# Hybrid mixer and mixture of experts on one core: six gates in other places, another order in routing, an extra slot of 64 places

## The chip, the cores and the metric

One core of a Trainium2 chip runs the whole program. The metric is the device time of one execution in microseconds (us); lower is better. The engines are named as in the profile: PE is TensorE (PEld its weight loads), DVE is VectorE, ACT is ScalarE, POOL is GpSimd, and SP issues most of the DMAs.

## The reference, cut to what matters

512 tokens of 1024 values go through a first block (which the change leaves alone) and a second one. The second has a mixer with three branches, each under a gate, and 16 experts of which each token uses two.

```python
def second_block(...):
    h = rms_norm(x, g_norm1) * (1 + sc1) + sh1
    x = x + gt1 * hybrid_mixer(h, ...)
    h2 = rms_norm(x, g_norm2) * (1 + sc2) + sh2
    return x + gt2 * hier_moe(h2, ...)

def hybrid_mixer(h, ...):                      # proj = h @ w_in, split into the parts below
    y_a = gmlp_branch(gelu(a_u), gelu(a_v), ...)  # u * (w_s @ layer_norm(v) + b_s), chunks of 128
    o_b = gla_scan(g_q, g_k, g_v, log_alpha)      # gated linear attention
    y_b = rms_norm(o_b, gla_norm_g) * silu(g_r)
    y_c = dsa_attention(q, k, d_v, d_iq, d_ik, d_iw, rel_bias)   # top 128 keys by an indexer
    up = einsum('nbse,ned->bsnd', [y_a, y_b, y_c], w_branch)
    gate = sigmoid(gates + b_branch_gate)         # 3 gates of 1024 columns, from h alone
    return sum(gate * up) @ w_out

def hier_moe(hf, ...):       # 4 groups of 4 experts: the best group, in it the best two experts
    for each expert:         # gate and up: 1024 -> 256 each, down: 256 -> 1024
        y += (silu(hf @ wg) * (hf @ wu) * weight) @ wd
```

## The kernel before, in words

**Products.** All large products are made in split precision: an fp32 operand is cut into a high half (a copy on ScalarE, L155 for weights) and a low half (a subtraction on VectorE, L156), and three matmuls add up hi*hi, lo*hi and hi*lo (L170 to L172). A product of 1024 rows and 128 columns for all 512 tokens, `gemm`, is 24 matmuls of 512 columns. `gemmA` (L971) is the same for 512 columns at once, with four PSUM tiles, one for each 128 tokens. A few small products are made in fp32, unsplit.

**Order.** Up to L1310 the order of the instructions on each engine is written by a planner when the program is built, from costs of its own and from the order in the program. From L1310 to the end of the experts the order on TensorE, VectorE and ScalarE is the program's own (`manual_schedule`); a call there that makes a weight's halves or a transpose's copy stands where it is written.

**Mixer.** The stretch runs from about 735 us to 1280 us of the span: the indexer and its top keys, the products for u, q and k, the product for v (`gemmA(A['wA'][0],ev_v)`, L1075), where `ev_v` normalises each block's rows (`gv`, L1074), and gMLP's mixing right behind it (`PE m L1078`). The attention follows (L1081 to L1105), a chain of small steps with little for TensorE. Then `merge(0)` adds gMLP's branch: for each of 8 column blocks d one gate (`gemm` of 24 matmuls, and a Tanh into the tile `th`, of which there are two) and one branch product of 12 matmuls, added into `merged[d]`. The gates need h alone, so the planner uses them, and with gMLP's branch products, as work for TensorE while the attention's chain runs. GLA comes next: its products, then seven levels of small matmuls (`gla_level`, L1140 to L1168), each behind a chain over VectorE (`kp`, `qp`) and ScalarE. `merge(2)` (the attention's branch) and `merge(1)` (GLA's) end the mixer, and the product with w_out's first half follows.

**Routing.** The second half of w_out goes by blocks of 128 tokens in the loop of L1345. Each block has four `product` calls of 6 matmuls; `x2half` adds them to x and sums the squares, `inverse` makes the inverse root, `turned`, `logits` and `added` bring the half's router logits of the block before, each over TensorE and another engine. `rows_out` writes a block's normalised rows, scaled by a2 (1 + sc2 times the weight), to `d_h2` in DRAM. For blocks 0 and 1, d_h2 has been filled with the shift sh2 long before (L1038), and POOL adds the rows by an accumulating DMA; for blocks 2 and 3, VectorE adds the shift row `sh2r` itself and SP writes them. After the loop the last block's three steps and its `rows_out` come, then the top-two choice, the ranks (`rps`), the one-hot tiles `Ak` and the token lists `idx`, all on VectorE with few matmuls. The gather (L1467) then fetches the first expert's rows from d_h2.

**Experts.** Each of 17 slots has 128 places: slots 0 to 15 are the experts' own, slot 16 is the extra one, for the expert with more than 128 tokens, if any. A slot transposes its gathered rows (L1473), splits them, makes the up products (`up_piece`, 4 pieces, 24 matmuls, 512 columns: 256 of the gate and 256 of up), Silu (L1488) times up, a transpose and the down products (`down`: 6 split matmuls and 2 fp32 ones), and adds its rows to the output by an indirect DMA of POOL's. Each expert's weights are 6 pieces of 512 KB, fetched by SP in the order of `todo` into 26 buffers (`slots`) as these come free, and split in the order of `pieces`, three pieces ahead of their use. What goes into the extra slot is found by `further` (slots 3 to 7) and `extra(0)` (slot 11). The last slots run in the order 15, 16, the end of slot 15 within slot 16's products. At the end a register `nx` decides whether a tail with six more slots runs (L1565), which is when more than one extra slot is needed.

## Time and profile before

| what | value |
|---|---|
| median of 3 runs | 1489.78 us (1485.41 to 1494.95) |
| profiled execution, its own time | 1490.69 us |
| its span in the trace | 1488.9 us |
| mean granted TensorE clock | 0.979 |
| TensorE (PE) busy | 1423.3 us, 96% |
| VectorE (DVE) busy | 1028.4 us, 69% |
| ScalarE (ACT) busy | 642.4 us, 43% |
| GpSimd (POOL) busy | 94.9 us, 6% |
| DMA | 226.16 MB, mean 152 GB/s |

The span runs from the first to the last instruction that the trace shows; the execution's own time is 1.8 us longer. Busy shares are means over the whole span. The granted clock is the share of TensorE's full clock that the chip let it run at. A line of the view of busy time by stretch has the stretch (start and end in us), its length, the busy us and the instructions of PE, PEld, DVE, ACT and POOL, then the granted clock, the DMA engines' busy share and their GB/s.

### The profile page before, as it was taken

The page shows a single profiled execution, that of the slowest core. Times are in us where ns is not written, and L with a number is a line of the kernel's source. Part 1 is how long each engine was busy: PE and PEld are TensorE (multiplying, and loading weights), DVE is VectorE, ACT ScalarE, POOL GpSimd, SP SyncE. Part 2 cuts the span into 40 slices and gives each one's busy share as a digit, 9 for nine tenths or more (in the row PEclk, how much of TensorE's full clock was granted, in tenths as well). Part 3 has the DMA queues.
Part 4 walks back from the last instruction along what each step waited for, and adds up shares of the span by engine and source line. Part 5 has one row for each costly group of instructions (what it writes and reads, how often), then busy time and mean ns, then how long its engine had stood idle before and what let it go on. Part 6 is the DMA issues. An engine that isn't in the chain of part 4 may idle for free. (4 is left out here: it accounts for less than half of the span.)

```text
span 1488.9 us, 22888 instructions
## 1 busy us (share of the span) xinstructions
PE 1423.3 (96%) x8863; PEld 1107.0 (74%) x8863; DVE 1028.4 (69%) x1948; ACT 642.4 (43%) x1045; POOL 94.9 (6%) x114
## 2 busy tenths in 40 slices
PE   9999998999999999999999989999899999599996
PEld 5777877677777787778777777777678887377774
DVE  6788977578777767544749867654544344789995
ACT  6554374234443443223443324463622333266663
POOL 0121000000000000000001000000000000123321
PEclk9999998999999999999999999999999999799999
DMA  5347234143556535553424211222044234499992
GB/s 215 134 154 251 85 112 133 66 142 124 167 177 212 183 115 188 172 170 114 146 99 140 92 57 50 64 95 80 23 167 138 92 127 165 142 391 362 331 342 58
DMA packets 78885, 226.16 MB, mean 152 GB/s; under 512 B 19571, under 2 KB 20211, under 8 KB 78771
## 3 DMA queue, kind: packets, MB, share of 16 engines
q1 hardware_dynamic: 68626, 201.79, 39.0%
q0 software_dynamic: 8992, 19.71, 4.8%
q10 hardware_dynamic: 1152, 3.15, 0.5%
q8 instruction: 71, 1.16, 0.3%
q14 instruction: 44, 0.35, 0.1%
HBM read 208.06 MB, written 27.03 MB: 158 GB/s over the span
## 5 line engine op out<-in xcount | busy, mean ns | idle before, releaser
L155 ACT ACTIVATE hi<-raw 128x1024 fp32r<-128x1024 f32 (+1 forms) x181 | 181.1, 1001 | 395.6 <-PE g L171 255.2
L156 DVE TENSOR_TENSOR lo<-raw,hi 128x1024 fp32r<-128x1024 f32 (+1 forms) x181 | 208.1, 1150 | 203.5 <-ACT hi L155 202.9
L172 PE MATMUL g<-bh,lo 128*128 128x512 f32 x376 | 152.4, 405 | 2.6 <-DVE lo L156 2.4
L170 PE MATMUL g<-bh,hi 128*128 128x512 f32 x376 | 152.1, 405 | 0.0
L171 PE MATMUL g<-bl,hi 128*128 128x512 f32 x376 | 150.3, 400 | 0.0
L170 PE MATMUL g<-hh,hi 128*128 128x512 f32 x336 | 133.1, 396 | 0.0
L172 PE MATMUL g<-hh,lo 128*128 128x512 f32 x336 | 132.7, 395 | 0.2 <-DVE lo L156 0.2
L171 PE MATMUL g<-hl,hi 128*128 128x512 f32 x336 | 132.6, 395 | 0.0
L172 PEld LDWEIGHTS g<-bh,lo 128*128 128x128 f32 x376 | 71.5, 190 | 22.6 <-DVE lo L156 4.1
L170 PEld LDWEIGHTS g<-bh,hi 128*128 128x128 f32 x376 | 71.7, 191 | 19.3 <-issue 2.4
L171 PEld LDWEIGHTS g<-bl,hi 128*128 128x128 f32 x376 | 71.4, 190 | 16.2 <-issue 0.2
L170 PE MATMUL g<-xh,hi 128*128 128x512 f32 x192 | 76.8, 400 | 0.0
L170 PEld LDWEIGHTS g<-hh,hi 128*128 128x128 f32 x336 | 63.3, 188 | 17.7 <-ACT hi L155 2.5
L172 PE MATMUL g<-xh,lo 128*128 128x512 f32 x192 | 76.4, 398 | 0.0
L171 PE MATMUL g<-xl,hi 128*128 128x512 f32 x192 | 76.2, 397 | 0.0
L172 PEld LDWEIGHTS g<-hh,lo 128*128 128x128 f32 x336 | 63.3, 188 | 15.5 <-DVE lo L156 0.6
L171 PEld LDWEIGHTS g<-hl,hi 128*128 128x128 f32 x336 | 63.3, 189 | 14.6
L885 DVE SCALAR_TENSOR_TENSOR acc<-raw,ca,acc 128x1024 f32<-128x1024 f32 x42 | 53.8, 1282 | 28.7 <-DMA raw<-in_wmod 28.4
L914 DVE SCALAR_TENSOR_TENSOR c<-g,vec,c 128x511 f32<-128x511 f32 x88 | 65.6, 745 | 1.1
L777 PE MATMUL g<-hi,fh 128*128 128x512 f32 x136 | 53.9, 396 | 0.0
L779 PE MATMUL g<-lo,fh 128*128 128x512 f32 x136 | 53.7, 395 | 0.0
L778 PE MATMUL g<-hi,fl 128*128 128x512 f32 x136 | 53.7, 395 | 0.0
(705 smaller groups left out, 3200.7 us busy)
## 6 DMA issues: line engine op xcount, KB each, us to landing
raw<-in_wexp SPq DMA_DIRECT2D x89, 512.0 KB, 13.2
raw<-in_win SPq DMA_DIRECT2D x72, 512.0 KB, 3.5
raw<-in_wmod SPq DMA_DIRECT2D x48, 512.0 KB, 4.1
raw<-in_wup SPq DMA_DIRECT2D x44, 512.0 KB, 4.3
raw<-in_wdn SPq DMA_DIRECT2D x22, 512.0 KB, 3.9
raw<-in_wout SPq DMA_DIRECT2D x16, 512.0 KB, 4.8
ws<-in_wexp SPq DMA_DIRECT2D x13, 512.0 KB, 14.3
raw<-in_wA SPq DMA_DIRECT2D x12, 512.0 KB, 3.9
```

The source lines that it names most:

```text
L155: S.activation(hi[:,:f],raw[:,:f],AF.Copy)
L156: V.tensor_tensor(lo[:,:f],raw[:,:f],hi.bitcast(F32)[:,:f],op=OP.subtract)
L170: PE.matmul(ps,hi[:,sl],xh[k],start=(k==0),stop=False)
L171: PE.matmul(ps,hi[:,sl],xl[k],start=False,stop=False)
L172: PE.matmul(ps,lo[:,sl],xh[k],start=False,stop=(k==n-1))
L777: PE.matmul(ps,xh[k][:,sl],w[kk][0],start=(k==0),stop=False)
L778: PE.matmul(ps,xl[k][:,sl],w[kk][0],start=False,stop=False)
L779: PE.matmul(ps,xh[k][:,sl],w[kk][1],start=False,stop=(k==2*n-1))
L885: else: V.scalar_tensor_tensor(acc,raw,ca[:,k:k+1],acc,op0=OP.mult,op1=OP.add)
L914: for k in (1,2): V.scalar_tensor_tensor(c[:,k:],ps[:,:512-k],Vc(f'fw{2-k}',i),c[:,k:],op0=OP.mult,op1=OP.add)
```

## The change

**Gates.** The Tanh tiles number four in place of two (GA+1), and each gate is a function of its own, `gate(n,d)`. `merge` makes the gates up to three blocks ahead of the branch product that uses them. Gates 0 to 2 of gMLP's branch are written between the product for v and gMLP's mixing; gates 0 to 2 of the attention's branch are written within GLA's levels, ahead of levels 0, 2 and 4.

**Routing.** `d_h2` is filled with the shift for all four blocks, and all four are then added by POOL's accumulating DMA; the row sh2r is not loaded. `rows_out` of the block before and `added` stand between the two halves of the last `product` call; the last block's `rows_out` is a scaling on ScalarE and stands ahead of its `added`; only block 3 is scaled by a2 ahead (`scaled`). 13 matmuls of 512 columns whose result nobody reads, `keep_going(13)`, stand behind the product that makes the token lists.

**The extra slot** has 64 places and is computed in fp32, with two halves of its columns in two column groups of TensorE's array (`rows64`, `up64`, `end64`, `act64`, `down64`), its weights unsplit. It stands between slots 14 and 15. Finding its expert begins a slot earlier (`further` in slots 2 to 6), and `extra(0)` is in slot 9. `keep_going(5)` stands ahead of the last slot's transposes. The tail runs when more than one extra slot is needed or an expert has more than 192 tokens, and then has seven slots, the first for the places behind the 64 of the extra slot.

```diff
-    mpool=pool('mp',bufs=2,stack=ph2)
+    GA=3
+    mpool=pool('mp',bufs=GA+1,stack=ph2)
...
+    gates={}
+    def gate(n,d):
+        ps=gemm(w2b(23+8*n+d),hh,hl)
+        gates[n,d]=th=mpool.tile([128,512],F32,name='th',tag='th'); S.activation(th,ps,AF.Tanh,bias=bgh[:,8*n+d:8*n+d+1],scale=0.5)
...
-            ps=gemm(w2b(23+8*n+d),hh,hl)
-            th=mpool.tile([128,512],F32,name='th',tag='th'); S.activation(th,ps,AF.Tanh,bias=bgh[:,8*n+d:8*n+d+1],scale=0.5)
+            for d2 in range(d,min(8,d+GA)):
+                if (n,d2) not in gates: gate(n,d2)
+            th=gates[n,d]
...
-    with tc.issue_after(oh_.ins): nc.sync.dma_start(d_h2[0:256,:],bass.AP(tensor=d_mod.tensor,offset=d_mod.offset+3072,ap=[[0,256],[1,1024]]))
+    with tc.issue_after(oh_.ins): nc.sync.dma_start(d_h2,bass.AP(tensor=d_mod.tensor,offset=d_mod.offset+3072,ap=[[0,512],[1,1024]]))
...
     gemmA(A['wA'][0],ev_v); next(kn_)
+    for d in range(GA): gate(0,d)
     for g in range(4):
...
     for li,n in enumerate((1,2,4,8,16,32,64)):
+        if li<2*GA and li%2==0: gate(2,li//2)
         for j in range(2): gla_level(li,n,j)
...
-    for i in range(4):
+    for i in (0,2,3):
         m=pe_.tile([128,1024],F32,name='modr',tag=f'modr{i}'); modr.append(m)
         nc.sync.dma_start(m,bass.AP(tensor=d_mod.tensor,offset=d_mod.offset+2048+1024*i,ap=[[0,128],[1,1024]]))
-    gt1r,sh2r,a2r,gt2r=modr
+    gt1r,a2r,gt2r=modr
...
+    def product(tb,ps,p,kks=(0,1)):
         sl=slice(tb*128,tb*128+128); hi,lo=wl1[p]
-        for kk in range(2):
+        for kk in kks:
...
-        if tb<2:
+        if tb<3:
             h=pw.tile([128,1024],F32,name='h2',tag='h2'); V.scalar_tensor_tensor(h,x1t[tb],v,a2r,op0=OP.mult,op1=OP.mult)
-            G.dma_start(d_h2[tb*128:tb*128+128,:],h,accum_op=OP.add)
         else:
-            h=blk[tb]['h']; V.scalar_tensor_tensor(h,h,v,sh2r,op0=OP.mult,op1=OP.add)
-            nc.sync.dma_start(d_h2[tb*128:tb*128+128,:],h)
+            h=blk[tb]['h']; S.activation(h,h,AF.Copy,scale=v)
+        G.dma_start(d_h2[tb*128:tb*128+128,:],h,accum_op=OP.add)
     for tb in range(4):
         ps=pg.tile([128,512],F32,name='g',tag='g')
         product(tb,ps,0); product(tb,ps,1)
         if tb: turned(tb-1)
         product(tb,ps,2)
         if tb: logits(tb-1)
-        product(tb,ps,3)
-        if tb: added(tb-1)
+        product(tb,ps,3,(0,))
+        if tb: rows_out(tb-1); added(tb-1)
+        product(tb,ps,3,(1,))
         x2half(tb,1,ps)
         nc.scalar.dma_start(out[tb*128:tb*128+128,:],x1t[tb])
-        if tb: rows_out(tb-1)
+        if tb==3: scaled(tb)
         inverse(tb)
-        if tb>=2: scaled(tb)
-    turned(3); logits(3); added(3); rows_out(3)
+    turned(3); logits(3); rows_out(3); added(3)
...
+    def keep_going(n):
+        w=pt()
+        for _ in range(n): PE.matmul(w,trib[:,:128],Ak[:,0:4,:].rearrange('p i s -> p (i s)'),start=True,stop=True)
+    keep_going(13)
...
+        mc=pe_.tile([128,1],F32,name='mc'); V.tensor_reduce(mc,cnt,axis=AX,op=OP.max)
+        V.scalar_tensor_tensor(mc,mc,192.5,pos[:,47:48],op0=OP.is_gt,op1=OP.add)
+        V.tensor_copy(ei[:,0:7],EQ[:,0,0:7]); V.tensor_copy(ei[:,7:8],mc)
...
-    for s_ in range(1,17): pieces+=[(s_,p) for p in range(4)]+[(s_-1,4),(s_-1,5)]
-    pieces[-6:]=[(16,0),(16,1),(15,4),(15,5),(16,2),(16,3),(16,4),(16,5)]
+    for s_ in range(1,15): pieces+=[(s_,p) for p in range(4)]+[(s_-1,4),(s_-1,5)]
+    pieces+=[(16,p) for p in range(4)]+[(14,4),(14,5),(15,0),(15,1),(16,4),(16,5)]+[(15,p) for p in range(2,6)]
...
+    def rows64(xg):
+        xf=pe2.tile([128,8,64],F32,name='xf',tag='xgl',bufs=1)
+        for hf in range(2):
+            ps=pt((128,4,64))
+            for kk in range(4): PE.transpose(ps[:,kk,:],xg[:64,(4*hf+kk)*128:(4*hf+kk)*128+128],ident[:64,:64])
+            S.activation(xf[:,4*hf:4*hf+4,:],ps,AF.Copy)
+        return xf
+    h64=lambda e: slice(64*e,64*e+64)
+    def up64(ps,xf,p,raw):
+        for kk in range(2):
+            k=2*p+kk
+            for e in range(2): PE.matmul(ps[h64(e),:256],xf[:,k],raw[:,kk*512+256*e:kk*512+256*e+256],start=(k==0),stop=(k==7))
+    def end64(ps,wcol):
+        u=sq_pool.tile([64,256],F32,name='u64',tag='sq',bufs=3); V.tensor_scalar(u,ps[64:,:256],wcol[:64],None,op0=OP.mult)
+        a=sq_pool.tile([64,256],F32,name='a64',tag='sq',bufs=3); S.activation(a,ps[:64,:256],AF.Silu)
+        V.tensor_tensor(a,a,u,op=OP.mult); return a
+    def act64(a):
+        pT=pt((128,2,64))
+        for f in range(2): PE.transpose(pT[:,f,:],a[:,f*128:f*128+128],ident[:64,:64])
+        af=pe2.tile([128,2,64],F32,name='af64',tag='afx',bufs=1); S.activation(af,pT,AF.Copy)
+        return af
+    def down64(af,raws,ix):
+        y=pe2.tile([128,1024],F32,name='ye',tag='ye',bufs=3); ps=psum()
+        for f in range(2):
+            for e in range(2): PE.matmul(ps[h64(e)],af[:,f],raws[f][:,512*e:512*e+512],start=(f==0),stop=(f==1))
+        for e in range(2): V.tensor_tensor(y[:64,512*e:512*e+512],ps[h64(e)],gt2r[h64(e),512*e:512*e+512],op=OP.mult)
+        G.indirect_dma_start(out=out,out_offset=bass.IndirectOffsetOnAxis(ap=ix,axis=0),in_=y[:64],in_offset=None,
+                             bounds_check=511,oob_is_err=False,compute_op=OP.add)
...
+    for e in range(14):
         O=None
-        if e<13: xgs.append(gather(idx[:,e+4:e+5]))
-        if e==3: fur=further()
-        if 3<=e<8: next(fur,None)
-        if e==11: xps=pm.tile([128,17,8],F32,name='m',tag='m'); O=extra(0,xps,16)
-        if e==8:
+        if e<11: xgs.append(gather(idx[:,e+4:e+5]))
+        else: xgs.append([lambda:gather(idx[:64,16:17],64),lambda:gather(idx[:,15:16]),lambda:None][e-11]())
+        if e==2: fur=further()
+        if 2<=e<7: next(fur,None)
+        if e==9: xps=pm.tile([128,17,8],F32,name='m',tag='m'); O=extra(0,xps,16)
+        if e==7:
             e0=nc.values_load(ei[0:1,0:1],min_val=0,max_val=15,engines=[ET.SP])
-            w0=[(A['wexp'][bass.ds(e0,1),p].rearrange('o p f -> (o p) f'),p==5) for p in range(6)]
-            todo+=w0[:2]+wx(15,(4,5))+w0[2:]
-        if e<16: ps=psum(); up_piece(ps,xin,0,piece(e+1,0))
+            w0=[(A['wexp'][bass.ds(e0,1),p].rearrange('o p f -> (o p) f'),True) for p in range(6)]
+            todo+=w0[:4]+wx(14,(4,5))+wx(15,(0,1))+w0[4:]+wx(15,range(2,6))
+        ps=psum(); up_piece(ps,xin,0,piece(e+1,0))
         aa=act_in(a)
-        if e<16:
-            for p in range(1,4):
-                if e==15 and p==2: down(aa,piece(e,4),piece(e,5),idx[:,e:e+1])
-                up_piece(ps,xin,p,piece(e+1,p))
-            a=up_end(ps,wcl[:,e+1:e+2])
+        for p in range(1,4): up_piece(ps,xin,p,piece(e+1,p))
+        a=up_end(ps,wcl[:,e+1:e+2])
         if O: placed(*O)
-        if e<15: xin=rows_in(xgs[e+2],e+2)
-        if e!=15: down(aa,piece(e,4),piece(e,5),idx[:,e:e+1])
+        xin=rows_in(xgs[e+2],e+2) if e<13 else rows64(xgs[15])
+        down(aa,piece(e,4),piece(e,5),idx[:,e:e+1])
         if O: infos(xps,16,17,wcl,idx)
+    ps=psum()
+    for p in range(2): up64(ps,xin,p,piece(16,p))
+    aa=act_in(a)
+    for p in range(2,4): up64(ps,xin,p,piece(16,p))
+    a=end64(ps,wcl[:,16:17])
+    xin=rows_in(xgs[16],15)
+    down(aa,piece(14,4),piece(14,5),idx[:,14:15])
+    ps=psum(); up_piece(ps,xin,0,piece(15,0)); af=act64(a)
+    up_piece(ps,xin,1,piece(15,1))
+    down64(af,(piece(16,4),piece(16,5)),idx[:64,16:17])
+    for p in range(2,4): up_piece(ps,xin,p,piece(15,p))
+    a=up_end(ps,wcl[:,15:16]); keep_going(5)
+    down(act_in(a),piece(15,4),piece(15,5),idx[:,15:16])
...
-    nx=nc.values_load(ei[0:1,7:8],min_val=0,max_val=7)
+    nx=nc.values_load(ei[0:1,7:8],min_val=0,max_val=8)
     with tc.If(nx>1):
         xps=pm.tile([128,17,8],F32,name='m',tag='m')
         wc2=pe_.tile([128,17],F32,name='wc2'); ix2=pe_.tile([128,17],U32,name='ix2')
-        for j in range(1,7): placed(*extra(j,xps,j))
```

## Rows read from the trace of the kernel before

**Rows 1.** The page, part 1: busy us of each engine, share of the span, instructions.
```profile
PE 1423.3 (96%) x8863; PEld 1107.0 (74%) x8863; DVE 1028.4 (69%) x1948; ACT 642.4 (43%) x1045; POOL 94.9 (6%) x114
```

**Rows 2.** Busy time by stretch, three of 50 us.
```profile
500.00:550.00 50.00, 50.00 (x217) 40.56 (x216) 35.92 (x42) 20.48 (x28) 0.00 (x0) 1.00 0.49 159
850.00:900.00 50.00, 45.48 (x217) 35.65 (x216) 34.63 (x97) 13.91 (x20) 0.00 (x0) 0.93 0.18 58
1350.00:1400.00 50.00, 50.00 (x224) 37.46 (x224) 48.20 (x67) 34.19 (x52) 17.76 (x10) 1.00 0.99 349
```

**Rows 3.** Waits of TensorE, 870 to 900 us: us in total, times, longest.
```profile
PE m L1078 <- DVE gv L1074: 3.9, 2, 2.8
PE g L170 <- ACT yh L186: 0.5, 1, 0.5
```

**Rows 4.** Busy time by stretch, cut at waits and clock steps.
```profile
891.60:898.40 6.80, 5.20 (x17) 4.36 (x17) 5.56 (x12) 2.93 (x5) 0.00 (x0) 0.50 0.12 48
1031.90:1064.40 32.50, 26.62 (x902) 19.48 (x902) 26.49 (x69) 19.10 (x55) 0.00 (x0) 0.95 0.04 12
1065.70:1069.10 3.40, 3.40 (x15) 2.46 (x16) 2.32 (x3) 1.94 (x5) 0.00 (x0) 0.50 0.32 107
1299.40:1304.60 5.20, 5.17 (x15) 4.00 (x16) 3.13 (x14) 2.64 (x4) 0.99 (x1) 0.50 0.89 289
1304.60:1309.00 4.40, 4.40 (x27) 3.35 (x26) 4.06 (x6) 3.12 (x4) 0.00 (x0) 1.00 1.01 397
```

**Rows 5.** Timeline of VectorE (start us, us, what), within 1049 to 1068 us.
```profile
1062.38 1.22 DVE L156 TENSOR_TENSOR lo<-raw,hi 128x1024 fp32r<-128x1024 f32 x1
```

**Rows 6.** Waits of TensorE, 1030 to 1066 us.
```profile
PE m L1138 <- issue: 2.3, 2, 2.0
...
PE g L172 <- DVE lo L156: 1.8, 1, 1.8
```

**Rows 7.** Timeline of all engines in routing; brackets: idle before, and its releaser.
```profile
1279.77 0.24 DVE L1329 TENSOR_REDUCE l<-m 128x20 f32<-128x80 f32 x1 [0.88 <-PE m L1328]
...
1280.41 0.69 DVE L1279 TENSOR_TENSOR g<-g,modr 128x512 f32<-128x512 f32 x1
...
1286.12 1.28 DVE L1343 SCALAR_TENSOR_TENSOR h<-h,nv,modr 128x1024 f32<-128x1024 f32 x1
...
1287.32 0.23 DVE L1365 TENSOR_REDUCE mx<-lg 128x20 f32<-128x80 f32 x1
...
1294.96 1.19 POOL L1467 DMA_INDIRECT xg<-d_h,idx  x1 [17.45 <-DVE idx L1408]
...
1299.43 1.94 PE L1473 MATMUL m<-cst,xg 128*128 128x128 f32 x8 [5.84 <-DMA xg<-d_h,idx]
```

**Rows 8.** Answer on the tile d_h, 1269 to 1278 us.
```profile
L1341 POOL DMA_DIRECT2D d_h<-h x2: 864/890/916, 1270.0 to 1276.6; - x2
...
DMA to landing us min/median/max: 5.0/5.1/5.2
```

**Rows 9.** Timeline of TensorE, 0 to 8 us.
```profile
1.20 5.28 PE L278 MATMUL m<-zb 128*128 128x512 bf16 x17 [1.20 <-DVE o L276]
```

**Rows 10.** Timeline of ScalarE, 1317 to 1329 us.
```profile
1317.48 0.38 ACT L1488 ACTIVATE a<-g 128x256 f32<-128x256 f32 x1 [1.87 <-PE g L1486]
...
1327.29 0.38 ACT L1488 ACTIVATE a<-g 128x256 f32<-128x256 f32 x1 [1.88 <-PE g L1486]
```

**Rows 11.** Timeline of TensorE, 825.7 to 827.2 us.
```profile
825.76 0.40 PE L172 MATMUL g<-bh,lo 128*128 128x512 f32 x1
826.08 1.06 PE L200 MATMUL m<-sq,cst 128*32 128x512 f32 x6
827.07 0.51 PE L170 MATMUL g<-bh,hi 128*128 128x512 f32 x1
```

**Rows 12.** Timeline of TensorE, 1471.5 to 1479 us.
```profile
1472.55 0.44 PE L1493 MATMUL m<-cst,a 128*128 128x128 f32 x2 [0.99 <-DVE a L1489]
```

**Rows 13.** Answer on line 1239 (fetches of expert weights), 1449 to 1451 us.
```profile
DMA to landing us min/median/max: 11.3/11.8/12.4
```

More of the change, by code (lines that the diff above doesn't have):

```diff
@@ L1230, in build @@
     nsl=[0]; ahead=[]; AS=[]
-    slots=[(rawm,'raw')]*NR+[(wr,'raw')]*4+[('pe',f'modr{i}') for i in (0,2,1)]+[(res_pool,f'res{i}') for i in range(4)]+[('AS',0),('AS',1),('AS',2),('AS',3),('pe2','rx0')]
+    slots=[(rawm,'raw')]*NR+[(wr,'raw')]*4+[('pe',f'modr{i}') for i in (1,0,2)]+[(res_pool,f'res{i}') for i in range(4)]+[('AS',0),('AS',1),('AS',2),('AS',3),('pe2','rx0')]
     NS=len(slots)
@@ L1242, in build @@
     todo=wx(0,range(4))
-    for e in range(1,16): todo+=wx(e,range(4))+wx(e-1,(4,5))
+    for e in range(1,15): todo+=wx(e,range(4))+wx(e-1,(4,5))
     merge(2,yq,False)
@@ L1311, in build @@
     blk=[{} for _ in range(4)]
-    def product(tb,ps,p):
+    def product(tb,ps,p,kks=(0,1)):
         sl=slice(tb*128,tb*128+128); hi,lo=wl1[p]
-        for kk in range(2):
+        for kk in kks:
             k=2*p+kk; c=slice(kk*512,kk*512+512)
@@ L1441, in further, with extra @@
         V.tensor_scalar(EQ[:,1,0:7],EQ[:,1,0:7],4096.0,None,op0=OP.add)
-        V.tensor_copy(ei[:,0:7],EQ[:,0,0:7]); V.tensor_copy(ei[:,7:8],pos[:,47:48])
-    def extra(j,ps,s):
+        mc=pe_.tile([128,1],F32,name='mc'); V.tensor_reduce(mc,cnt,axis=AX,op=OP.max)
+        V.scalar_tensor_tensor(mc,mc,192.5,pos[:,47:48],op0=OP.is_gt,op1=OP.add)
+        V.tensor_copy(ei[:,0:7],EQ[:,0,0:7]); V.tensor_copy(ei[:,7:8],mc)
+    def extra(j,ps,s,upper=False):
         eq=pe2.tile([128,16],F32,name='eq',tag='eq'); V.tensor_scalar(eq,C3('iota')[:,0:16],EQ[:,0,j:j+1],None,op0=OP.is_equal)
@@ L1447, in extra @@
         cc=pe2.tile([128,4],F32,name='xcc',tag='xcc'); V.tensor_reduce(cc,c,axis=AX,op=OP.add)
-        V.tensor_scalar(cc,cc,EQ[:,1,j:j+1],None,op0=OP.subtract)
+        V.tensor_scalar(cc,cc,EQ[:,1,j:j+1],64.0 if upper else 0.0,op0=OP.subtract,op1=OP.subtract)
         tx=st_pool.tile([128,4,8,16],F32,name='tx',tag='ss',bufs=1); V.tensor_tensor(tx,tk.rearrange('p t e c -> p t c e'),eq[:,None,None,:].to_broadcast([128,4,8,16]),op=OP.mult)
@@ L1461, in ensure, with gather @@
         while len(done)<min(n,len(pieces)):
-            s_,p=pieces[len(done)]; done.append(wnext(p==5 or (s_<NW and p<4)))
+            s_,p=pieces[len(done)]; done.append(wnext(p==5 or s_==16 or (s_<NW and p<4)))
     def piece(s_,p):
         n=pieces.index((s_,p)); ensure(n+1+LA); return done[n]
-    def gather(ix):
+    def gather(ix,n=128):
         xg=pe2.tile([128,1024],F32,name='xg',tag='xg',bufs=3)
-        G.indirect_dma_start(out=xg,out_offset=None,in_=d_h2,in_offset=bass.IndirectOffsetOnAxis(ap=ix,axis=0),bounds_check=511,oob_is_err=False)
+        G.indirect_dma_start(out=xg[:n],out_offset=None,in_=d_h2,in_offset=bass.IndirectOffsetOnAxis(ap=ix,axis=0),bounds_check=511,oob_is_err=False)
         return xg
@@ L1540, in build @@
     for p in range(3): V.tensor_tensor(tk[:,:,:,2+p],bw[:,0:4,p,:],bw[:,4:8,p,:],op=OP.add)
-    for e in range(17):
+    for e in range(14):
         O=None
-        if e<13: xgs.append(gather(idx[:,e+4:e+5]))
-        if e==3: fur=further()
-        if 3<=e<8: next(fur,None)
-        if e==11: xps=pm.tile([128,17,8],F32,name='m',tag='m'); O=extra(0,xps,16)
-        if e==8:
+        if e<11: xgs.append(gather(idx[:,e+4:e+5]))
[4 more added lines that the diff above has]
+        if e==7:
@@ L1567, in build @@
         wc2=pe_.tile([128,17],F32,name='wc2'); ix2=pe_.tile([128,17],U32,name='ix2')
-        for j in range(1,7): placed(*extra(j,xps,j))
-        infos(xps,1,7,wc2,ix2)
-        for j in range(1,7):
+        for j in range(7): placed(*extra(j,xps,j,upper=j==0))
+        infos(xps,0,7,wc2,ix2)
+        for j in range(7):
             ej=nc.values_load(ei[0:1,j:j+1],min_val=0,max_val=15,engines=[ET.SP])
```

4 lines of the change are left out of this document (3 added, 1 removed).

## The prediction

> **What bounds the kernel now.** I read the page first, then the table of busy time by stretch, then TensorE's waits in the stretches that the diff touches, then the timeline of routing, and last the granted clock in stretches cut at the waits.
>
> TensorE is busy for 96% of the span [rows 1]: it sets the time, and only where it stands idle, runs at the lower clock or has less to do can this change gain. In a full stage it starts 217 matmuls in 50 us, 0.23 us each, without a gap; in 850 to 900 it is busy for 45.5 of 50 us at a mean clock of 0.93 [rows 2]. The experts' stage is full too, but there the DMA share is 0.99 and VectorE is busy for 48.2 of 50 us, so two others are near their limit.
>
> **A, gates ahead of gMLP's mixing.** Before the mixing TensorE has run out of work that is ready: it waits 3.9 us in two pieces for the normalised values (DVE gv) and 0.5 us for the first half of the split input [rows 3]. The clock falls while it stands, and from 891.6 to 898.4 only half of it is granted [rows 4]; of the 5.2 us that TensorE is busy there some 2.2 would not be needed at full clock (I take a little under half). So 6.6 us can be had. The change moves two more gates' products ahead of the mixing (one stands there already): 24 matmuls of 0.23 us each, 5.5 us a gate, 11 us of cover for a wait of under 8 us. They are the same matmuls, taken from the attention's filler, of which enough is left: six more gates' worth of the branch's products follow after. What is queued behind them: each gate brings a 128x1024 subtraction to DVE (1.22 us [rows 5]), in front of the mixing's own additions, and a Tanh to ScalarE; the gates' results wait in four buffers in place of two. I take 5.5 us, with ends at 0 (the order on TensorE is written by a planner from its own costs, and may put the mixing in front of the gates) and 8 (attention's own waits go too).
>
> **B, three gates within GLA's levels.** From 1031.9 to 1064.4 TensorE is busy for 26.6 of 32.5 us, so 5.9 us are idle, and the clock halves twice; one such stretch is shown, 3.4 us with 15 instructions [rows 4]. Of the idle time 1.8 us is a wait for one weight's low half and 2.3 us is put down to issue, with nothing waited for that the profile shows [rows 6]. The low half is late because the planner put its subtraction behind the levels' work: DVE makes it at 1062.38 [rows 5]. Gates written between the levels come ahead of the later levels in the program's order, so their subtractions should come earlier, and 72 matmuls (16.6 us) are more than the hole. Upper end: 5.9 idle and some 2.5 of clock, 8.4 us. Lower end 0: the issue time may be none that filler ends, and a gate of 5.5 us in front of a level delays the level's chain on DVE. I take 4 us, just under half, since under half of the idle time is a wait that filler surely ends.
>
> **C, routing.** This part is written out by hand for TensorE, VectorE and ScalarE, so its order is known. Now the three small steps of added(2) stand ahead of the last half-block (1279.77 to 1280.41), and rows_out costs 1.28 us each for blocks 2 and 3, the latter's at 1286.12, right ahead of routing's first step at 1287.32; the gather starts at 1294.96 and TensorE resumes at 1299.43 [rows 7]. After the change added(2) is done before the last half-block's products end: 0.7 us. rows_out(2) lies in DVE's wait ahead of it, and rows_out(3) goes to ScalarE. Then DVE has scaled(3) and inverse(3) to do while logits(3) runs its five steps over TensorE and ScalarE, some 2.9 us from the half-block's end in the same timeline; added(3) follows it. Routing then starts 1.9 us earlier than by today's order, 2.6 us with the 0.7. What is new behind it: blocks 2 and 3 are now written by an accumulating DMA on POOL's queue, which lands 5.1 us after its issue, and the gather must find them there [rows 8]. The last is issued at about 1285 (a 1.0 us scaling on ScalarE after the inverse), lands at about 1290, and the gather would start at 1292.4: covered by some 2.3 us, and each us beyond that is paid. The filling of d_h2 grows from 1 to 2 MB at 783 us and one modulation row of 0.5 MB is no longer loaded; weights land there more than 15 us ahead of their use, so I cost both at nothing.
>
> The 13 matmuls of keep_going fill TensorE's queue while the gather is out. At half clock 512 columns take 0.43 us, so they end 5.6 us after their start at the latest, before the gather has landed, and delay nothing. What they may buy is in the two last windows: from 1299.4 to 1304.6 TensorE got half the clock and did 15 instructions in 5.2 us, and then 27 in 4.4 us [rows 4]. At the start of the program 17 matmuls of the same size on zeros took 5.28 us, 0.31 each on the mean, between the 0.43 of 1.2 GHz and the 0.21 of 2.4 GHz [rows 9]: the clock rose while they ran. Full clock would give back up to 2.6 us of that stretch; DVE's weights for the first slot take some of that. 1.5 us, ends 0 and 2.6. C: 4.1 us.
>
> **D, the extra slot of 64 places.** A slot's period is 9.81 us, from one Silu to the next [rows 10]. TensorE fills it: 24 matmuls up (5.5 us), 6 matmuls and two fp32 ones down (3.2 us), transposes the rest (1.1 us). What an fp32 product costs in a column group shows in the row norms: three products of 512 columns in three groups start together and the next matmul follows 0.99 us later [rows 11]; they share the time of one, 0.90 us after 0.09 for the switch of layout (0.32 in place of 0.23 to the first of them). The new slot has 8 pairs of 256 columns (3.6 us), 2 pairs of 512 (1.8 us), half the transposes (0.55 us) and some 6 switches (0.5 us): 6.5 us, so 3.3 less. Its five splits (1.22 us each on DVE, 1.06 on ScalarE) go as well, which nothing waits for. keep_going(5) at the end takes 1.1 us and the wait that it fills is 0.99 us [rows 12]: 0.1 us lost, since TensorE is done before any clock falls. The extra's bookkeeping on DVE moves from slot 11 to slot 9 unchanged.
>
> The Trainium skill, "TensorEngine Tiling (Array Packing)", Key Properties, speaks against this slot: changing the tiling mode drains TensorE. The trace agrees that there is a price, the 0.09 us above, and no run here shows it for 64 columns; the page gives no length, and at five times that price the slot would still gain 1 us.
>
> **The sum.** 5.5 + 4 + 4.1 + 3.3 = 16.9 us off the profiled execution's 1490.69 us: 1473.8. The median of the three runs is 0.9 us lower, their spread 9.5 us. I predict 1473 us.
>
> **The rivals.** *First: filling brings nothing.* The planner's costs put the gates where they already ran, or each gate's subtraction delays the chain that it covers. For it: it left a converted weight behind the levels for 12 us. Against it: ahead of the mixing the wait is longer than its own additions and the gates need no result of the attention. A and B at about 0 leave 7.4 us: 1483.
>
> *Second: the halves don't run side by side.* If the two column groups take turns, the slot needs 16 times 0.45, 4 times 0.90 and the transposes, 11.4 us, 1.6 more than today. Against it: the three groups of rows 11. 4.9 us of the sum go: 1478.
>
> *Third: the weights bound the end.* Each expert weight lands 11.8 us after its issue near the end [rows 13], with the DMA queues always full; its conversion follows some 4 to 6 us later there. Starting TensorE 1.5 us sooner against the same stream and taking 3.3 us from slot 16 uses up most of that. By my count the last four weights land 1 to 2 us before they are needed; if DMA is slower by that, C's clock and D are paid back: 1478.
>
> *Fourth, slower: the conditional tail runs.* The new test asks for the tail when an expert has more than 192 places, and the tail is then 7 slots, each of at least 9.81 us as nothing is prefetched: 69 us, to 1542. It decides at one expert's load of 193. Against it: no instruction of the tail stands in the trace, and the reference's own router on its inputs of seed 0 gives no expert more than 131.
>
> **How the numbers follow.** The forecast has 0.62; the rivals in order 0.18, 0.07, 0.09 and 0.03; the rest is a slowdown that I don't see, 0.01. The range for 8 in 10 is 1463 to 1484: its low end takes A and B near their upper ends, its high end the first rival with a little noise. About 1% is what measuring can tell here, 14.9 us, so 1474.9 is the bound of faster. The forecast lies just beyond it, and of the 0.62 I count seven tenths as faster (0.43), with three tenths of the second and third rivals (0.05) and a little of the first (0.02): 0.50. Slower has 0.04, and within 1% the rest, 0.46.
>
> **What the next profile would show.** A right: the two waits for gv gone, no half clock at 891 to 898. B right: fewer than 3 us idle in the levels and a low half made well before the level that follows. C right: routing's first step 2.6 us nearer to the last block's products, 13 dummies ending before the gather lands, the clock full in the first slot. D right: pairs of 64-column matmuls starting together, some 6.5 us for that slot. Wrong: a wait of the gather for d_h2, ScalarE or TensorE waiting for a weight's DMA in the last slots, or new waits in the attention, whose filler is now thinner.

## The result and the profile after

The changed kernel takes 1477.97 us (median of 6 runs, 1472.49 to 1479.89) against 1491.9 us (median of 6, 1485.41 to 1494.95): the ratio is 0.9909, with a 95% interval of 0.9889 to 0.9929. That is 14 us less where 17 had been forecast; whether it is more than the 1% that the prediction asked of "faster" (0.50 for that, 0.46 for within 1%) the interval leaves open. The profiled execution is the fastest of the six, 1472.49 us with a span of 1470.7, so the two traces differ by more, 18.2 us. Where they differ is read from the same events in both timelines (us from the span's start):

| event | before | after | difference |
|---|---|---|---|
| transposes at the first block's end (L834) | 718.31 | 716.50 | -1.8 |
| last block's transposes in routing | 1281.97 | 1267.22 | -14.8 |
| routing's first step on VectorE | 1287.32 | 1270.61 | -16.7 |
| first slot's transposes | 1299.43 | 1282.80 | -16.6 |
| Silu of slot 0 | 1309.85 | 1291.55 | -18.3 |
| Silu of slot 1 | 1317.48 | 1301.20 | -16.3 |
| Silu of slot 13 | 1439.07 | 1420.66 | -18.4 |
| TensorE's end | 1477.00 | 1456.14 | -20.9 |
| end of the span | 1488.91 | 1470.71 | -18.2 |

The first line is no part of the change: the first block's instructions are the same, and in the profiles of the thirteen kernels with any part of the change this row starts between 716.5 and 721.8 us. It is not the last row of L834, as the expectations below call it: more follow, the next 8.2 us later in either kernel, so it marks the same point in all of them. 12.9 us come from the mixer (0.7 of them from routing's blocks), 1.9 from the rest of routing; within the experts the difference swings by 2 us from slot to slot, they gain 4.2 up to TensorE's end, and give 2.7 back after it. The page, part 1, of the changed kernel (before: [rows 1]):

```profile
PE 1416.2 (96%) x8885; PEld 1098.0 (75%) x8887; DVE 1017.5 (69%) x1941; ACT 636.0 (43%) x1038; POOL 94.2 (6%) x116
```

TensorE's waits in the changed kernel, first 870 to 902 us, then 1020 to 1066 (before: [rows 3, 6]):

```profile
PE g L170 <- ACT yh L186: 0.7, 1, 0.7
...
PE m L1167 <- DVE qp L1157: 1.5, 1, 1.5
PE m L1145 <- issue: 1.0, 1, 1.0
PE m L1193 <- DVE df L1191: 0.4, 1, 0.4
```

The two waits for gv are gone, and so is the one for the low half in GLA's levels. In its place stands 1.5 us for `qp`, the levels' own chain. The clock still falls twice there (1041 to 1045 and 1058 to 1062 us), as it did before. Busy time by stretch, changed kernel (before: [rows 2, 4]):

```profile
850.00:900.00 50.00, 49.28 (x248) 39.86 (x243) 31.54 (x88) 14.16 (x20) 0.00 (x0) 1.00 0.21 73
...
1282.80:1290.60 7.80, 7.32 (x41) 5.54 (x42) 6.28 (x17) 5.57 (x7) 0.99 (x1) 1.00 0.88 311
1290.60:1294.00 3.40, 1.71 (x11) 1.15 (x10) 3.22 (x8) 3.23 (x5) 0.99 (x1) 1.00 1.03 417
1294.00:1297.40 3.40, 3.40 (x10) 2.62 (x10) 2.61 (x6) 0.78 (x3) 0.00 (x0) 0.50 1.02 413
```

In 850 to 900 us TensorE does 248 matmuls where it did 217, at full clock. The first slot (from 1282.8) runs at full clock too, but half clock comes back in the second slot, behind a stretch in which TensorE was busy for half of the time. Routing in the timeline (before: [rows 7]):

```profile
1269.77 1.15 ACT L1350 ACTIVATE h<-h,nv 128x1024 f32<-128x1024 f32 x1 [0.34 <-DVE nv L233]
...
1270.61 0.24 DVE L1372 TENSOR_REDUCE mx<-lg 128x20 f32<-128x80 f32 x1
...
1271.21 0.84 POOL L1351 DMA_DIRECT2D d_h<-h  x1 [6.08 <-ACT h L1350]
...
1277.54 3.93 PE L1415 MATMUL m<-Ak,trib 128*128 128x512 bf16 x11 [0.22 <-issue]
...
1278.19 1.25 POOL L1482 DMA_INDIRECT xg<-d_h,idx  x1 [6.14 <-DVE idx L1419]
```

The last block's rows are scaled on ScalarE while VectorE goes on, POOL adds them to d_h2 at 1271.2, and the gather at 1278.2 waits for the list `idx` alone. The 13 dummies (11 in this row) end at 1281.5, 1.3 us ahead of the gathered rows. The extra slot on TensorE:

```profile
1434.27 1.95 PE L1536 MATMUL g<-raw,xf 128*64 128x256 f32 x16
1436.15 0.44 PE L1508 MATMUL m<-cst,a 128*128 128x128 f32 x2
1436.52 1.95 PE L1536 MATMUL g<-raw,xf 128*64 128x256 f32 x16
...
1445.46 0.40 PE L1501 MATMUL g<-lo,xgh 128*128 128x512 f32 x1
1445.79 1.94 PE L1549 MATMUL g<-raw,af 128*64 128x512 f32 x8
1447.65 0.50 PE L1499 MATMUL g<-hi,xgh 128*128 128x512 f32 x1
1447.99 0.40 PE L1500 MATMUL g<-hi,xgl 128*128 128x512 f32 x1
```

Each fp32 matmul stands as two records: the 16 in a row are the 8 matmuls, or 4 pairs, of half of the up products. They take 1.88 us from start to start, 0.47 a pair, where the working had 0.45 for one such product alone. The halves run side by side. Now the end: the last scatter's rows and the scatter from the timeline, and its landing from the answer on its line, first before, then in the changed kernel:

```profile
1477.04 0.69 DVE L1507 TENSOR_TENSOR ye<-g,modr 128x512 f32<-128x512 f32 x1 [0.86 <-PE g L1506]
1478.26 1.54 POOL L1508 DMA_INDIRECT out<-ye,idx  x1 [5.07 <-DVE ye L1507]
```

```profile
DMA to landing us min/median/max: 3.9/3.9/3.9
```

```profile
1453.28 1.43 POOL L1551 DMA_INDIRECT out<-ye,idx  x1 [5.03 <-DVE al L1511]
...
1456.17 0.69 DVE L1522 TENSOR_TENSOR ye<-g,modr 128x512 f32<-128x512 f32 x1 [0.86 <-PE g L1521]
1458.03 1.55 POOL L1523 DMA_INDIRECT out<-ye,idx  x1 [3.32 <-PEq L1619]
```

```profile
DMA to landing us min/median/max: 5.6/5.6/5.6
```

The last rows are ready at 1456.86, their scatter leaves at 1458.03 and lands 5.6 us later. Before, the last scatter left 0.5 us after its rows (1478.26 after 1477.73) and landed in 3.9.

### The profile page after: what moved, and what is told of

Its sections match the earlier page's. It is cut to its first block, busy times and chain, and to the rows that moved or that the text cites. A ratio compares the mean times of both kernels' runs of the same rounds, so it can differ in the third digit from the quotient of the medians.

```text
span 1470.7 us, 22899 instructions
## 1 busy us (share of the span) xinstructions
PE 1416.2 (96%) x8885; PEld 1098.0 (75%) x8887; DVE 1017.5 (69%) x1941; ACT 636.0 (43%) x1038; POOL 94.2 (6%) x116
```

## Experiments

Each is the changed kernel with the edit shown, cut where it says `...`. "The stretch" is that from the transposes at the first block's end (the table's first line) to the last block's transposes in routing; "slot time" counts from the first slot's transposes. Both leave the first block out.

**The early gates, one set or both undone.** Behind each line stand the kernels that drop it.

```diff
-    for d in range(GA): gate(0,d)                               # u_a, u_look
-        if li<2*GA and li%2==0: gate(2,li//2)                    # u_b, u_look
```

> The changed kernel without the three gates written ahead of gMLP's mixing; the gates then stand in the merge loop, still up to three ahead of their branch product. Measured by the stretch from the last transposes of the first block (716.5 us in the changed kernel) to the last block's transposes in routing (1267.2): 550.7 us there, 563.7 before the change. Theory (the gates cover the wait for the normalised values and keep the clock up): the two waits for gv come back with 3 to 4 us, the half clock behind them with some 2 us, and the stretch is 556 to 557 us, the time 5 to 6 us longer than the changed kernel's. Rival (what gained was the look-ahead in the merge loop, and the attention's waits take back what the mixing loses): 551 to 553 us, the time within 2 us.

> The changed kernel without the three gates within GLA's levels; merge(2) makes them. Same stretch, 550.7 us in the changed kernel. Theory (the gates fill TensorE's idle time in the levels and bring the late weight half forward): idle time of TensorE from the first level to the products behind them goes from about 3 us back to about 6 us, a second half-clock stretch of 3.4 us comes back, and the stretch is 554 to 556 us. Rival (the filler only moves the waits, the levels' own chain over VectorE and ScalarE sets their time, and the gates are paid there instead of in merge(2)): 550 to 552 us.

> The changed kernel with neither set of explicit early gates, but with the look-ahead of three in the merge loop and the four Tanh tiles kept. The stretch from the first block's last transposes to the last block's transposes in routing was 550.7 us in the changed kernel, 554.0 and 553.9 with one set of early gates undone, 563.9 with everything of the gates undone. Theory (the look-ahead and its two more tiles bring some 7 us by themselves, since the planner can then put gates of gMLP's branch into the wait ahead of the mixing; the explicit calls bring 3 us each on top): 556 to 558 us, no wait for gv over 1 us. Rival (either set is enough for most of the gain, and with neither the waits are all back): 562 to 564 us, both waits for gv there.

**All that concerns gates undone, and the same with four Tanh tiles.** u_ab drops `gate`, the look-ahead in `merge` and GA; u_tiles is u_ab with

```diff
-    mpool=pool('mp',bufs=2,stack=ph2)
+    mpool=pool('mp',bufs=4,stack=ph2)
```

> The changed kernel with none of the gates' moves: two Tanh tiles, each gate right ahead of its branch product; routing and the extra slot stay changed. Same stretch. Theory (the moves of the six gates are all of the gain): 562 to 563 us, and this is the sum of what the two single undos cost. Rival (the look-ahead in the merge loop brings something by itself): the two single undos sum to some us less than this one costs. Third: if each of the two moves covers the other's loss, the sum of the single ones is larger than this one's cost.

> The kernel with the changed routing and extra slot, with the merge loop as it was before the change (each gate right ahead of its branch product, no early gates), but with four Tanh tiles in place of two. The stretch from the first block's last transposes to the last block's transposes in routing was 554.7 us with the look-ahead and four tiles, 563.9 with neither, 550.7 to 553.7 in kernels with the whole change of the gates. Theory (it is the number of Tanh tiles that kept the planner from putting gates into the wait ahead of the mixing): 554 to 557 us and no wait for gv over 1 us. Rival (the planner keeps to the program's order, and the look-ahead in the loop, not the tiles, is what moves the gates): 562 to 564 us, with both waits for gv.

| kernel | stretch, us | ratio to before |
|---|---|---|
| before (0.7 us of it the old routing's) | 563.7 | 1 |
| u_ab, no change of the gates | 563.9 | 0.9971 (0.9951 to 0.9990) |
| u_tiles, four tiles alone | 562.5 | 0.9987 (0.9969 to 1.0005) |
| u_look, look-ahead and four tiles | 554.7 | 0.9938 (0.9913 to 0.9963) |
| u_a, without the gates ahead of the mixing | 554.0 | 0.9917 (0.9892 to 0.9943) |
| u_b, without the gates in GLA's levels | 553.9 | 0.9917 (0.9892 to 0.9941) |
| the changed kernel | 550.7 | 0.9909 (0.9889 to 0.9929) |
| six more kernels below with its gates and routing | 549.9 to 553.7 | |

The look-ahead in the merge loop, with its four tiles, brings some 9 us (whether it would with fewer tiles was not run). Both explicit sets together add some 4 by the median of the seven kernels that have them (550.9), and either of them alone under 1. Since these seven, which differ in nothing ahead of routing, spread over 3.9 us, the effect of the explicit sets is not resolved, single or together; that of the look-ahead is. By time, too, only u_ab and u_tiles stand clear of the changed kernel: the intervals of all the others overlap with its.

Of the expectations, u_a's theory missed: at 554.0 us it lies between theory and rival, and no wait for gv came back. In u_b the late low half came back, as expected,

```profile
PE g L172 <- DVE lo L156: 1.8, 1, 1.8
```

but with one half-clock stretch in GLA, not two. In u_ab the rival was right: the two single undos cost 6.5 us, this one 13.2. u_look came out better than its theory. That tiles were what kept the planner back, my theory for u_tiles, fell: 1.4 us less than u_ab is within the spread. Waits of TensorE ahead of the mixing in u_tiles, then the Tanhs of the first gates in u_tiles (L991) and in u_look (L988):

```profile
PE m L1078 <- DVE gv L1074: 3.0, 2, 2.8
PE g L170 <- ACT yh L186: 0.9, 1, 0.9
```

```profile
891.48 0.67 ACT L991 ACTIVATE th<-g,bgh 128x512 f32<-128x512 f32 x1
909.12 0.67 ACT L991 ACTIVATE th<-g,bgh 128x512 f32<-128x512 f32 x1
```

```profile
890.74 0.67 ACT L988 ACTIVATE th<-g,bgh 128x512 f32<-128x512 f32 x1
898.64 0.67 ACT L988 ACTIVATE th<-g,bgh 128x512 f32<-128x512 f32 x1
904.80 0.68 ACT L988 ACTIVATE th<-g,bgh 128x512 f32<-128x512 f32 x1
```

With the old loop one gate comes ahead of the wait, however many tiles there are, because the next thing in the program is a branch product that needs the mixing's result. With gates 1 and 2 written ahead of that product the planner puts them into the wait. Busy time, 870 to 905 us, first u_ab, then u_look:

```profile
870.00:905.00 35.00, 30.49 (x144) 24.62 (x142) 27.50 (x81) 9.95 (x16) 0.00 (x0) 0.90 0.15 46
```

```profile
870.00:905.00 35.00, 34.46 (x174) 27.85 (x172) 29.38 (x83) 12.59 (x21) 0.00 (x0) 1.00 0.15 46
```

30 matmuls more in the same 35 us, 6.9 us at 0.23 each: 4 us of waits and the lost clock. Of the other 2.3 us, 1.7 is a half-clock stretch of 3.4 us fewer in GLA (two against three). That may be no part of the gates' gain: kernels alike ahead of routing have one there (i_order, i_tabsplit) or two.

**The old routing order**, with the dummies kept: `rows_out`, `product`, the loop, the shift row and d_h2's filling as before.

> The changed kernel with the old routing order (rows_out behind x2half, blocks 2 and 3 with the shift row on VectorE and written by SP, all of product in one piece); the 13 matmuls and the extra slot stay. Measured from the last block's transposes to the first slot's transposes of gathered rows: 15.6 us in the changed kernel, 17.5 before. Theory (the time to the gather is VectorE's chain, and 1.9 us of it were moved off plus 0.7 us in the blocks): 17.4 to 17.6 us there, and 2.5 us more in all. Rival (the gather waits for the last rows in d_h2 or for the DMA either way): 15.6 to 16.2 us.

From the last block's transposes to the first slot's it took 17.6 us (15.6 in the changed kernel), and 0.7 us more in the blocks ahead: 2.7 us in all. The ratio, 0.9928 (0.9905 to 0.9951), can't tell it from the changed kernel's. By the profile the theory holds; the gather is set by VectorE's chain in either order.

**No dummies.**

```diff
-    keep_going(13)
```

> The changed kernel without the 13 matmuls behind the token lists. From the first transposes of gathered rows to the Silu of slot 0 it took 8.75 us with them and 10.42 before the change; to the Silu of slot 1 18.40 and 18.05. Theory of the prediction (they buy the clock of the first slot): 10.4 us to slot 0, and the later slots 1.5 us later than in the changed kernel. Rival (they only move the half-clock stretch from the first slot to the second): 10.4 us to slot 0, but 17.9 to 18.5 us to slot 1 and no change behind it. The time itself: 0 to 2 us longer, under what this measurement can tell.

Slot times of the Silus and of TensorE's end:

| | slot 0 | slot 1 | slot 9 | slot 11 | TensorE's end |
|---|---|---|---|---|---|
| before | 10.42 | 18.05 | 96.49 | 116.10 | 177.57 |
| changed | 8.75 | 18.40 | 96.51 | 118.36 | 173.34 |
| u_look (with dummies) | 8.75 | 16.85 | 94.97 | 118.41 | 173.38 |
| u_dummy | 10.35 | 17.98 | 96.09 | 119.50 | 174.49 |

The dummies give slot 0 1.6 us. A half-clock stretch of 3.4 us is left all the same: in the changed kernel in slot 1, in u_look and u_dummy on the way to slot 11's Silu, each behind waits (in slot 1 of 0.9 and 0.8 us, in the others of 1.9). The changed kernel has the same wait of 1.9 us at the same place (to 1390.0) and stays at full clock behind it; why is not shown. At TensorE's end the dummies are worth 1.15 us. The rival described slot 1 rightly, the theory the end; the ratio (0.9922, 0.9896 to 0.9948) can't tell them.

**The old extra slot**, with its place, bookkeeping and tail, and no dummies at the end.

> The changed kernel with the old extra slot of 128 places, its old place, bookkeeping and tail, and without the 5 matmuls at the end. From the first transposes of gathered rows TensorE ended after 173.3 us in the changed kernel and 177.6 before; the end of the span followed 14.6 and 11.9 us later. Theory (the new slot saves TensorE 2.4 us, and the wait of the last scatter for the one before it, which the short slot brings closer, gives part of it back at the end): TensorE ends 175.5 to 176.5 us after the transposes, and the end follows 12 us later, so that the whole is within 1 us of the changed kernel. Rival (the later end is only a slower landing of that one run): the end follows 13 to 15 us later here too, and the whole is 2 to 3 us longer.

TensorE ends at a slot time of 179.5, later than the theory's 175.5 to 176.5, and the span at 191.7, 3.8 us behind the changed kernel's where the theory had 1. u_d has two half-clock stretches of 3.4 us, at 1417 and 1465 us, that the changed kernel has not, and such stretches are in other places from kernel to kernel; at half of their length they make 3.4 of the 6.2 us between the two ends of TensorE, and leave 2.8 for the slot. Behind TensorE's end the theory was right, and the rival wrong: it takes 12.2 us, 2.4 less than with the new slot. By time the new slot's gain is not shown: u_d's ratio is 0.9916 (0.9892 to 0.9941). Its last scatter, and the landing:

```profile
1470.44 1.54 POOL L1519 DMA_INDIRECT out<-ye,idx  x1 [6.37 <-DVE ye L1518]
```

```profile
DMA to landing us min/median/max: 4.1/4.1/4.1
```

The later end was no accident of one run: it is 11.9 and 12.2 us in the two kernels with the old slot, 13.9 to 15.5 in the ten that have the new one between slots 14 and 15.

**The extra slot's rows to another tensor.**

```diff
+    d_side=dten('d_side',[512,1024])
...
-        G.indirect_dma_start(out=out,...,in_=y[:64],...)     # in down64
+        G.indirect_dma_start(out=d_side,...,in_=y[:64],...)
```

> The changed kernel with the extra slot's rows added into another DRAM tensor in place of the output (so the extra slot's rows are missing from the output). The accumulating scatter of slot 15 then follows that of slot 14 and no longer waits for the extra slot's. In the changed kernel TensorE's end is followed by 14.6 us, and the last scatter is issued 1.2 us after its rows are ready. Theory (the chain of scatters is the end's limit): the last scatter is issued within 0.4 us of its rows, and the end is 1 to 1.5 us nearer to TensorE's end. Rival (the scatter waits for POOL itself or for the order on its queue, not for the other's landing): no change, 14 to 15 us.

```profile
1460.61 0.69 DVE L1522 TENSOR_TENSOR ye<-g,modr 128x512 f32<-128x512 f32 x1 [0.86 <-PE g L1521]
1461.58 1.55 POOL L1523 DMA_INDIRECT out<-ye,idx  x1 [5.01 <-DVE ye L1522]
```

The last scatter leaves 0.28 us after its rows (1461.58 after 1461.30; 1.17 in the changed kernel), as the theory said. The end follows TensorE's by 13.9 us, 0.6 less than in the changed kernel, where the theory had 1 to 1.5; by that much the ends of kernels with the same last slots differ too. It still takes 5.8 us to land. By time (0.9896, 0.9860 to 0.9933) it is not told from the changed kernel. The packets from the last scatter on differ, first before, then in the changed kernel (two or three of them are on the instruction queues):

```profile
DMA packets 146, 0.04 MB, mean 3 GB/s; under 512 B 141, under 2 KB 141, under 8 KB 144
```

```profile
DMA packets 147, 0.18 MB, mean 14 GB/s; under 512 B 108, under 2 KB 108, under 8 KB 144
```

The last scatter of the old order has 3 packets of 4096 bytes among its 144 (an extra slot with 3 real rows), that of the new one 36 (slot 15).

**The extra slot last.** The order 14, 15, 16; slot 15's down products within the extra slot's.

```diff
...
+    up64(ps,xin,0,piece(16,0)); aa=act_in(a); up64(ps,xin,1,piece(16,1))
+    down(aa,piece(15,4),piece(15,5),idx[:,15:16])
+    for p in range(2,4): up64(ps,xin,p,piece(16,p))
+    a=end64(ps,wcl[:,16:17]); keep_going(5)
+    down64(act64(a),(piece(16,4),piece(16,5)),idx[:64,16:17])
```

> The changed kernel with the slot of 64 places last, behind slot 15, in place of between 14 and 15; slot 15's down products stand between the halves of the last slot's up products. In the changed kernel and its variants TensorE's end is followed by 14 to 15.5 us, 12 before the change: the last scatter waits 0.3 to 1.8 us for the landing of the one before it, and takes 5.6 to 5.9 us to land with 36 rows of 4 KB, where before the change the last one carried 3 rows and took 3.9. Theory (the last scatter's rows and the chain of scatters set the end): the last scatter lands 4 us after its issue, and the span from the first slot's transposes to the end, 187.3 to 188.9 us in the variants with the slot between, is 2 to 4 us shorter. Rival (the slot is so short that the scatter of slot 15 is still out when its rows are ready, and the wait takes back what the landing gains): within 1 us.

```profile
1454.88 1.55 POOL L1523 DMA_INDIRECT out<-ye,idx  x1 [5.21 <-DVE u L1538]
...
1458.33 1.39 DVE L1550 TENSOR_TENSOR ye<-g,modr 64x512 f32<-64x512 f32 x2 [2.87 <-PE g L1549]
1461.37 1.44 POOL L1551 DMA_INDIRECT out<-ye,idx  x1 [4.94 <-PEq L1614]
```

The last scatter leaves 1.65 us after its rows (1461.37 after 1459.72): slot 15's had left at 1454.88, takes 5.7 us to land, and was still out. For the last one's landing this trace has no figure; the same scatter takes 3.4 us in i_all below. The span ends at a slot time of 186.7, 1.2 us less than in the changed kernel, where the theory had 2 to 4 and the rival under 1: both had a part. The ratio, 0.9921 (0.9898 to 0.9944), shows no gain.

**The function table earlier, and the extra slot's bookkeeping in parts.** In the changed kernel ScalarE's rows at slot 0's Silu and TensorE's behind it:

```profile
1290.25 1.28 ACT L1503 ACT_TABLE_LOAD   x1
1291.55 0.38 ACT L1503 ACTIVATE a<-g 128x256 f32<-128x256 f32 x1
1291.83 1.08 ACT L186 ACTIVATE xgh<-m 128x512 fp32r<-128x512 f32 x2
...
1292.47 0.51 PE L1499 MATMUL g<-hi,xgh 128*128 128x512 f32 x1 [0.86 <-ACT xgh L186]
...
1293.81 0.65 PE L1500 MATMUL g<-hi,xgl 128*128 128x512 f32 x1 [0.83 <-DVE xgl L187]
```

```diff
     ensure(3)
+    sil=pe_.tile([128,1],F32,name='sil'); S.activation(sil,rm[:,0:1],AF.Silu)
-        if e==9: ...; O=extra(0,xps,16)
+        if 7<=e<=9: next(parts)          # the same instructions in three parts
```

> The changed kernel with two additions: a Silu of one column in the time in which ScalarE waits for the gathered rows, so that the load of its function table (1.28 us at slot 0's Silu, ahead of slot 1's split input) is done there; and extra(0) in three parts in slots 7, 8 and 9 in place of at once in slot 9. Per slot, the changed kernel takes 9.66 us to the second Silu, 11.93 to the eleventh and 9.76 otherwise. Theory (the table load is what makes TensorE wait 0.86 and 0.83 us in slot 1, and the 3.5 us of extra(0) on VectorE what makes it wait 1.9 us in slot 10, and the half-clock stretch of 3.4 us follows one of these waits): the waits in slot 1 fall to under 0.6 us in all, the one in slot 10 to under 0.4, there is no half-clock stretch between 1290 and 1400, and TensorE's end comes 4 to 5 us sooner after the first transposes. Rival (VectorE is full in each slot, so that the parts only spread the delay; DMA landing is the bound behind it): under 1.5 us.

TensorE ends at a slot time of 171.6, 1.7 us sooner: near the rival's 1.5, not 4 to 5. The wait in slot 10 is gone (9.89 us where it was 11.93) and so is slot 1's half clock. The table is loaded while ScalarE waits for the gather, but in slot 1 TensorE now waits 1.4 us for VectorE's low half: the wait moved to the next engine. From slot 14's Silu to slot 15's it took 21.6 us in place of 20.3, since ScalarE stands before weights that have not landed, and slot 15's input is queued behind them. The waits of ScalarE for weights, 1390 to 1442 us, in this kernel:

```profile
ACT ws L1315 <- DMA raw<-in_wexp: 6.7, 3, 4.2
ACT hi L1315 <- DMA raw<-in_wexp: 1.2, 1, 1.2
```

The ratio to before is 0.9895 (0.9874 to 0.9916).

**Both together** (the bookkeeping in four parts).

> The changed kernel with the early Silu, extra(0) in four parts (slots 7 to 10) and the slot of 64 places last: the two kernels before this one together. From the first slot's transposes TensorE ended after 173.3 us and the span after 187.9 in the changed kernel, after 171.6 and 186.0 with the early Silu and extra(0) in parts, after 173.1 and 186.7 with the slot last. Theory (the gains are in different places and add): the end 184.8 us after the transposes, 3 us less than in the changed kernel. Rival (the experts' weights arrive no sooner, and what is gained ahead of the last slots is paid back in waits for them, as ScalarE's two waits of 4.2 and 2.2 us in the second of the two kernels suggest; the chain of scatters does the same): 186 us or more. The time: 0 to 4 us under the changed kernel's, which this measurement may just tell.

The rival was right: the span ends at a slot time of 188.1. TensorE ends at 171.6, but the last scatter leaves 4.5 us after its rows. The chain of scatters in its timeline:

```profile
1450.03 1.55 POOL L1537 DMA_INDIRECT out<-ye,idx  x1 [7.00 <-DMA out<-ye,idx]
...
1456.78 1.55 POOL L1537 DMA_INDIRECT out<-ye,idx  x1 [5.21 <-DMA out<-ye,idx]
1457.48 1.39 DVE L1564 TENSOR_TENSOR ye<-g,modr 64x512 f32<-64x512 f32 x2 [2.86 <-PE g L1563]
1463.37 1.44 POOL L1565 DMA_INDIRECT out<-ye,idx  x1 [5.03 <-DVEq L1631]
```

6.7 and 6.6 us lie between one scatter and the next, while TensorE ends 1.7 us sooner. The ratio of i_all, 0.9886 (0.9868 to 0.9905), overlaps with the changed kernel's: no version that is shown to be better came out.

## Why the prediction was right, point by point

**A.** The waits, the half clock and their size were read rightly: 4.4 us of waits and 2.2 of clock were there to be had. The step "the change moves two more gates' products ahead of the mixing" named the wrong line. The look-ahead in `merge` does it, 9.2 us from u_ab to u_look (5.5 taken, 8 the upper end); without the explicit calls u_a has no wait for gv either.

**B.** 4 us were taken; what this set gives alone is not resolved. The late low half went, as said, and is back in u_b. "Fewer than 3 us idle" came out at 3.1, half of it the chain's own wait. Of the clock nothing was gained: two half-clock stretches before, two after, and one in u_b without these gates. The first rival is right that the levels' chain sets a part of their time that no filler ends, but A and B together are 12.3 us of the profile where it had about 0.

**C.** 2.6 us were taken, 2.5 came out in the timeline, 2.7 by u_c. The accumulating DMAs cost nothing: POOL's last addition is issued 7 us ahead of the gather. The dummies: 1.5 taken, 1.6 in slot 0, 1.15 at TensorE's end; that the clock could fall again in slot 1 was not in the working.

**D.** From slot 13's Silu to TensorE's end it takes 35.5 us after and 37.9 before: 2.4 us, where the sum had 3.3 less 0.1. The halves run side by side, so the second rival falls. The slot's own rows take 6.5 us, as forecast, but the 6.5 of the working had the changes of layout in it: its transposes take 0.9 us where it had 0.55, and six times the matmul at a change starts its successor after 0.32 to 0.34 us where it is 0.23 elsewhere (1445.46 to 1445.79, 1447.65 to 1447.99). With these 0.6 us the slot costs 7.1, which leaves 2.7 of the 3.3; the rest is not accounted for. The Trainium skill, "TensorEngine Tiling (Array Packing)", Key Properties, has the drain at a change of tiling mode; the trace agrees with some 0.1 us a change, as the working took. **The step that failed** is that D was worked out to TensorE's end and no further ("TensorE is done before any clock falls"): the time from there to the end of the span was put at no change without a reason. It grew by 2.7 us: the short slot brings the last scatter to within 4.8 us of the one before, and puts a scatter of 36 rows at the end in place of one of 3. By the rows 0.6 of it is waiting (1.17 against 0.53 us), 1.7 landing (5.6 against 3.9), and 0.3 comes after the landing. e_scatter takes the wait away and keeps the landing; u_d, with the old slot, has the short landing, 4.1. The Trainium skill, "DMA: Bandwidth & Descriptors", Rules for kernel authors, tells an accumulating DMA to wait for the semaphore of an earlier one on the same bytes; that is the order which the traces show, and e_scatter, with another tensor, has no such wait.

**Sum.** By the profiles, with the first block left out: 12.3 for A and B (9.5 forecast), 2.5 for routing (2.6), 1.6 for the experts (4.8): 16.4 against 16.9. That the total is so near is luck: the mixer's surplus and the experts' lack cancel. The medians differ by less, 13.9 us, for the profiled execution after is the fastest of its six, with the shortest first block of all the profiles; against 13.9 the forecast is 3 us too much.

**The third rival** (the weights bound the end) has not come yet: in the changed kernel ScalarE waits 2.4 us for weights (2.2 the longest) and TensorE for none of it. In i_tabsplit, 1.7 us faster, it begins to: the 21.6 us to slot 15's Silu, in place of 20.3. The tail did not run.

## What to carry to other kernels

Where a planner follows the program's order, filler must be written ahead of the first thing that blocks; a look-ahead in the loop brought 9.2 of the mixer's 12.3 us here, and more buffers alone nothing that shows. Work out a saving to the last DMA's landing, not to the busiest engine's end: ask which transfer comes last, how many rows it carries, and whether it must wait for the one before. A wait that is ended on one engine can come back on the next: without the table load slot 1 waited 1.4 us for VectorE's low half.

## What was not expected of the hardware

- The landing of an accumulating scatter of equally many packets (144), last in its kernel, goes with how many of them carry rows: 3.9 and 4.1 us with 3 rows of 4 KB (before, u_d), 5.6 and 5.8 with 36 (the changed kernel, e_scatter). With 80 packets and 3 rows it is 3.4 (i_all).
- The load of ScalarE's function table stands as a row of its own, 1.28 us. The Trainium skill, "ScalarE activation tables: per-element evaluation and per-set limits", What a function is on this engine, gives 1283 ns; the trace agrees.
- Slots 2 to 9 take 9.76 us each on the mean in the changed kernel and most of its variants, and 9.81 in the kernel before, u_d, i_tabsplit and i_all, with the same products. Why stays open.
